# A third pair of blocks of K of u and v in seven products, the gating norm moved behind the scores, the spatial product behind half of the first gate

## The chip, the cores and the metric

The kernel runs on one core of one Trainium2 chip. The metric is the device time of one execution in microseconds (us). The kernel before took 512.1 us (median of 3 runs, 511.56 to 512.21). The engines are named as the profile names them: PE (TensorE: matmuls; PEld, its weight loads), DVE (VectorE), ACT (ScalarE), POOL (GpSimd) and SP (SyncE, which issues the DMAs).

## The reference

One residual block of a decoder on 256 tokens of width 1024, in f32: a SwiGLU FFN at half weight (hidden width 2816), a mixing layer, a second SwiGLU FFN at half weight, and a final RMS norm. The change lies in the mixing layer:

```python
n = rmsnorm(h, mix_norm)
z = n @ w_in                      # q, k, v (512 each), u and gv (512 each)
attn = moba_attention(q, k, v)    # 256 tokens, one block: causal softmax attention, 8 heads of 64
zg = gelu(z[..., 1536:])          # u, gv
gm = u * (W_s @ layernorm(gv) + b)   # per group of 64 channels, inside chunks of 128 tokens
gates = sigmoid(n @ w_gate + b_gate)
merged = gates[..., :D] * (attn @ w_branch_attn) + gates[..., D:] * (gm @ w_branch_gmlp)
h = h + merged @ w_out
```

In the kernel's units "u" is the first half of zg, "v" is the attention's v, and "gv" is the second half of zg, which gets the layer norm and the spatial product.

## The kernel before, in words

**Products.** Every weight matrix is read from HBM in f32 and split on the chip into a high part (a cast on ACT, L266) and a low part (a subtraction on DVE, L268). A product of a 128x128 block of activations with 512 columns of weights is then three matmuls into one PSUM bank (`mm3`, L261 to L263). Weights come in *units* of 1 MB, fetched by SP as two halves of 512 KB into 7 raw buffers (`fetch`, L186) and split into one of 5 split buffers (tag "w"). `split_to(n)` splits up to unit n and sets the fetches of the halves behind it going; `unit(i, ahead)` makes sure that the units up to i + ahead are split. The program's order in ACT, DVE, PE and SP is the order of the code in this part of the kernel (L758 on stands under `in_order()`, and PE's and SP's order is manual everywhere). So a split that is written earlier in the code stands earlier in DVE's queue.

**Seven products for eight.** For 2 blocks of K, 2 halves of the tokens and 2 halves of 512 columns, 8 products are needed. `seven` (L393) makes them from 7, in the manner of Strassen and Winograd: sums of quarters of the weights (`quarter_sums`, L200: four additions on DVE) and sums of blocks of the activations (`make_forms`, L411: four DVE operations, a cast on ACT, a low part on DVE). The weights of such a pair are two units: "single" (3 blocks of 512 columns) and "sums" (4 blocks), so 7 blocks are split from the 4 that are fetched. `chunk_pair` (L421) runs the pairs of a product, puts their results together (L437 to L441), and its `rest` multiplies the blocks of K that are left in the plain way (L443 to L453).

**The stretch around the change**, in PE's order: the first halves of K for q, k and gv (the second half of h is still on its way); their second halves; u and v together, of whose 8 blocks of K four are in two pairs (`PAIR_UV`) and four are plain, in units "u" and "v"; the scores of the attention; the spatial product (L925); then the eight units of the gate weights (four products g of two units each, `chunk(mg, ...)`). Beside it DVE and ACT split the units ahead, turn q and k by 32x32 transposes and a way through DRAM (L851 to L855, `from_way`), norm gv (`layer_norm`, L972, written ahead of u and v), add the masks (L876), and do the softmax (L879 to L907), whose probabilities go through DRAM as well (`to_keys`, `by_keys`). Later come the attention's product (`attend`, L960), the branch products with the gates (`merge`, L1077), whose results go through DRAM to the output projection (`down_features`, L1111).

**Queues.** While q and k are on their way, `hold[0] = 2 * mg` keeps SP from fetching gate weights; after the reads of the turned q and k it is lifted (L999), and the gate fetches stand behind those reads in SP's queue. A raw buffer comes free when the low part (or the last quarter sum) that reads it is done.

Of the kernel before, what the change touches and what calls it, by code (L numbers as in the profile page):

```python
# [18 lines left out]
P = 128  # L19
D = 1024  # L20
S = 256
# [25 lines left out]
WARM = 17  # L47
PAIR = {"f1": 6, "f2": 6}
PAIR_K = 3
PAIR_UV = 2  # L50


@with_exitstack
def block_kernel(ctx, tc, t, out):
# [84 lines left out]
    units.extend((name, i) for i in range(2) for name in ("q", "k", "gv"))  # L139
    muv = len(units)  # L140
    units.extend(("uvs", i, what) for i in range(PAIR_UV) for what in ("single", "sums"))
    units.extend([("u", 0), ("v", 0)])
    mg = add_units("gate", 8)
    mb = len(units)
    units.extend([("bg", 0), ("ba", 0), ("bg", 1), ("ba", 1)])
# [42 lines left out]
    def split_half(later=False):  # L188

        i, hf = divmod(done_to[0], 2)  # L190
        if hf == 0:
            unit_tile(i)
        fetch_to(done_to[0] + RAW)
        done_to[0] += 1
        if kind(i):
            return quarters(i, hf)
        w, sl = parts[i], half(i, hf)
        return split(w[:, sl, 0, :], w[:, sl, 1, :], raws.pop((i, hf)), later)

# [7 lines left out]
        nc.vector.tensor_add(second[:, 0], first[:, 0], d)  # L207
        nc.vector.tensor_add(second[:, 1], second[:, 0], c)

    def quarters(i, hf):  # L210

        w = parts[i]
        if kind(i) == "single":
            r = raws[i, hf].rearrange("p one (n c) -> p (one n) c", c=512)
            r, to = (r, w[:, 1:3]) if hf else (r[:, :1], w[:, :1])
        else:
            if hf == 0 and (i, 0) not in raws:
                quarter_sums(i)
            r, to = raws.pop((i, hf)), w[:, 2 * hf:2 * hf + 2]
        return split(to[:, :, 0, :], to[:, :, 1, :], r)  # L220

    def split_to(n):
        while done_to[0] < 2 * min(n, len(units)):
# [41 lines left out]
    def split(hi, lo, src, later=False):  # L265
        nc.scalar.copy(hi, src)  # L266
        def rest():
            nc.vector.tensor_sub(lo, src, hi.bitcast(F32))  # L268
        return rest if later else rest()
# [151 lines left out]
            between()  # L421
        low()

    def chunk_pair(name, at, nT, forms, ahead):


        acc, shared = {}, {}

        def tokens_of(k, j):
            return tuple(p[:, j * P:(j + 1) * P] for p in block_of(nT, k))  # L430

        for i in range(len(forms)):
            seven(name, at + 2 * i, i, tokens_of, acc, shared, forms[i], i == len(forms) - 1, ahead)
        p1, p5, p6, p7 = (shared[n,] for n in (1, 5, 6, 7))
        to = [sump.tile([P, NT, 512], F32, tag="sum", name=f"{name}{e}") for e in range(2)]
        (c00, c10), (c01, c11) = ([x[:, j] for j in range(NT)] for x in to)
        nc.scalar.copy(c00, p1)  # L437
        nc.vector.tensor_add(c01, p6, c00)
        nc.vector.tensor_add(c10, p7, c01)
        nc.vector.tensor_add(c11, p5, c10)  # L440
        nc.vector.tensor_add(c01, p5, c01)  # L441

        def rest(e, ahead=ahead):  # L443
            at_rest, near = at + 2 * len(forms), KB - 2 * len(forms)
            w = unit(at_rest + e * (near == 4), ahead)
            for k in range(near):
                for j in range(NT):
                    product(acc, name, (j, 512 * e), tokens_of(KB - near + k, j),
                            tuple(w[:, (2 * e + k) % 4 if near == 2 else k, two, :] for two in range(2)), k == near - 1)
            for j in range(NT):  # L450
                x = to[e][:, j]
                (nc.vector.tensor_sub if e else nc.vector.tensor_add)(x, acc[j, 512 * e], x)
            return [to[e][:, j] for j in range(NT)]  # L453
        return rest
# [303 lines left out]
    with in_order():  # L758
# [54 lines left out]
            if n == len(f1d) - 3:  # L813
                norm_parts(0)

        uv_forms = act.tile([P, 2, 4, 2, P], F32R, tag="nD", name="uvforms")
        uv_normed = sump.tile([P, 4, S // 32, 32], F32, tag="sum", name="uvnormed")
        hold[0] = 2 * mg
        psq = chunk(mq, nT2, "q", 0, [0], apart=3)
# [4 lines left out]
        psk = chunk(mk, nT2, "k", 0, [0], apart=3)  # L824
        for k in range(4):
            nc.scalar.activation(uv_normed[:, k], h_block(k), AF.Identity, scale=gain2[:, k:k + 1])
        for i in range(PAIR_UV):
            rest = split_half(True)
            make_forms(lambda j, k: uv_normed[:, 2 * i + k, 4 * j:4 * j + 4, :], uv_forms[:, i], f"uvform{i}", rest)
        norm_parts(1)  # L830
        psgv = chunk(mgv, nT2, "gv", 0, [0], apart=3)
        mixed = act.tile([P, 2 * FB, S], F32, tag="aT", name="mixed")
        mix_a, mix_b = mixed[:, :FB], mixed[:, FB:]
# [135 lines left out]
                                 start=False, stop=True)  # L969
            split(aoT[:, hp, 0, :], aoT[:, hp, 1, :], po[:, :S])  # L970

        def layer_norm(j):  # L972
            st = small.tile([P, 6], F32, tag="st", name=f"st{j}")
            nc.vector.bn_stats(st, gv[:, j, :])
            mvr = small.tile([P, 2], F32, tag="mvr", name=f"mvr{j}")
            nc.vector.bn_aggr(mvr, st)
            ve = small.tile([P, 1], F32, tag="ve", name=f"ve{j}")
            nc.vector.tensor_scalar(ve, mvr[:, 1:2], EPS, None, op0=ALU.add)
            r = small.tile([P, 1], F32, tag="lnr", name=f"lnr{j}")
            nc.gpsimd.tensor_tensor(r, ve, nhalf, op=ALU.pow)  # L980
            nc.vector.scalar_tensor_tensor(gv[:, j, :], gv[:, j, :], mvr[:, 0:1], lng, op0=ALU.subtract, op1=ALU.mult)
            nc.vector.scalar_tensor_tensor(gv[:, j, :], gv[:, j, :], r, lnb, op0=ALU.mult, op1=ALU.add)


        nc.sync.dma_start(lng, t["ln_g"].to_broadcast([P, GW]))
        nc.sync.dma_start(lnb, t["ln_b"].to_broadcast([P, GW]))
        chunk(mq, nT2, "q", 0, [1], psq, 3, DEEP)
        turn_qk(0, psq)
        chunk(mk, nT2, "k", 0, [1], psk, 3, DEEP)
# [1 line left out]
        quarter_sums(muv + 3)  # L991
        turn_qk(1, psk)
        nc.sync.dma_start(by_token(qk_way[1]), qk_turned[1])
        q_back = tmp.tile([P, S // 32, P], F32, tag="back", name="qback", bufs=1)
        from_way(q_back, qk_way[0])
        qk = act.tile([P, 2, 4 * S], F32, tag="nC", name="qk")
        kT = qk[:, 1].rearrange("p (q c) -> p q c", q=S // 32)
# [4 lines left out]
        for j in range(NT):  # L1002
            nc.scalar.activation(gv[:, j, :], psgv[j], AF.Gelu_apprx_tanh, scale=rs2[j])

        for j in range(NT):
            lows = [split_half(True) for _ in range(2)]
            layer_norm(j)
            for low in lows:
                low()
        qT = qk[:, 0].rearrange("p (k t) -> p k t", k=4)  # L1010
        nc.scalar.copy(qT.rearrange("p k (q c) -> p q k c", c=32), q_back.rearrange("p q (k c) -> p q k c", c=32))
        uv = chunk_pair("uv", muv, nT2, [uv_forms[:, i] for i in range(PAIR_UV)], DEEP)
        psu = uv(0)
        for j in range(NT):
            nc.scalar.activation(ut[:, j, :], psu[j], AF.Gelu_apprx_tanh, scale=rs2[j])
        psv = uv(1, ALONE)

        scores(0)
        scores(1)
        spatial()  # L1020
        psg = chunk(mg, nT2, "g", 0, [0])
        nc.sync.dma_start(gates[:, 0, :], t["b_gate"].to_broadcast([P, 2 * D]))

        sooner = act.tile([P, 2, 2, 512], F32, tag="nD", name="sooner")
# [172 lines left out]
def _packed(inputs):  # L1197
# [5 lines left out]
    def by_half(w):  # L1203
        return w.reshape(2, KB // 2, P, -1).transpose(0, 2, 1, 3)
# [30 lines left out]
    def paired(units, c):  # L1235
# [13 lines left out]
        "f1d": down1.reshape(FB, P, 2, 512)[REST].transpose(2, 0, 1, 3).reshape(PLAIN, 4, P, 512).transpose(0, 2, 1, 3),  # L1249
        "f2d": rows(a["ffn2_w_down"][0][hidden]),  # L1250
        "q": by_half(w_in[:, :AW][:, four]), "k": by_half(w_in[:, AW:2 * AW][:, four]),
        "v": by_half(w_in[:, 2 * AW:3 * AW])[1:],
        "u": by_half(w_in[:, 3 * AW:3 * AW + GW])[1:], "gv": by_half(w_in[:, 3 * AW + GW:]),
        "uvs": rows(np.concatenate([w_in[:, 3 * AW:3 * AW + GW], w_in[:, 2 * AW:3 * AW]], 1))[:PAIR_UV],
        "gate": chunks(a["w_gate"][0][order]),
        "ba": cols(a["w_branch_attn"][0], AW, 512), "bg": cols(a["w_branch_gmlp"][0][four], GW, 512),
# [26 lines left out]
```

## Time and profile before

| | |
|---|---|
| median of 3 runs | 512.1 us (511.56 to 512.21) |
| the profiled execution | 511.55 us, span of its instructions 509.8 us |
| PE busy | 502.2 us (99%), 2314 matmuls |
| DVE busy | 459.4 us (90%) |
| ACT busy | 313.1 us (61%) |
| POOL busy | 11.4 us (2%) |
| mean granted TensorE clock | 0.996 |
| HBM read | 113.26 MB, 248 GB/s over the span with the writes |

Times in the trace are us from the first instruction of the span. Busy PE is modelled: a matmul of 512 columns is shown with 389 ns and overlaps the next, so the distance between two starts is what one costs in a row. The stage table gives busy time of each engine between two times; what is missing to the stage's length is idle time.

### The profile page before, as it was taken

What the parts mean: (1) busy time and instruction counts of PE and PEld (TensorE: products, weight loads), DVE (VectorE), ACT (ScalarE), POOL (GpSimd) and SP (SyncE); (2) the same over time, 40 slices, a digit from 0 to 9 for tenths busy, and PEclk for the clock granted to TensorE, in tenths of its full rate; (3) what the DMA queues carried; (4) which work ended last, traced back from release to release, by engine and by line L of the source; (5) the groups of instructions that cost most, each with busy time, mean ns of one, the idle gap of its engine ahead of it and who ended that gap; (6) DMA issues with size and microseconds to landing.
All of it is one profiled execution on the core that took longest, in us unless ns stands there. A gap on an engine that the chain in (4) does not pass through costs nothing.

```text
span 509.8 us, 6828 instructions
## 1 busy us (share of the span) xinstructions
PE 502.2 (99%) x2314; PEld 416.9 (82%) x2314; DVE 459.4 (90%) x674; ACT 313.1 (61%) x452; POOL 11.4 (2%) x25
## 2 busy tenths in 40 slices
PE   8999999999999999999999999999999999999995
PEld 6888888888888888888888888888888888888884
DVE  6898999999997988999995657998989999999995
ACT  7985549646573775866984603767726656565533
POOL 0010000001000010000000000001000000000001
PEclk9999999999999999999999999999999999999998
DMA  8998587798865878497899655927799659998502
GB/s 316 375 328 343 140 294 236 279 307 279 242 208 204 256 309 299 139 358 244 291 284 315 225 164 172 314 97 265 256 278 302 214 150 273 351 333 242 184 1 82
DMA packets 63986, 126.82 MB, mean 249 GB/s; under 512 B 11728, under 2 KB 36816, under 8 KB 63824
## 3 DMA queue, kind: packets, MB, share of 16 engines
q1 hardware_dynamic: 63664, 126.08, 74.7%
q8 instruction: 18, 0.29, 0.2%
q10 hardware_dynamic: 288, 0.31, 0.2%
q14 instruction: 16, 0.13, 0.1%
HBM read 113.26 MB, written 13.11 MB: 248 GB/s over the span
## 4 chain that ended last, share of the span: by engine, by line
PE 97%; DMA 1%; DVE 0%; issue 0%; ACT 0%; POOLq 0%; DVEq 0%; POOL 0%; ACTq 0%
PE f L261 12%; PE f L262 12%; PE f L263 12%; PE accdown L263 4%; PE accdown L262 4%; PE accdown L261 4%; PE acch L262 4%; PE acch L261 4%; PE acch L263 4%; PE acc L235 3%; PE g L261 3%; PE g L262 3%; PE g L263 3%; PE acc L240 1%; PE accuv L262 1%; PE accuv L263 1%
## 5 line engine op out<-in xcount | busy, mean ns | idle before, releaser
L268 DVE TENSOR_TENSOR w<-raw,w 128x1024 fp32r<-128x1024 f32 (+1 forms) x176 | 198.2, 1162 | 10.1 <-ACT w L266 9.8
L266 ACT CAST w<-raw 128x1024 fp32r<-128x1024 f32 (+1 forms) x176 | 169.3, 1007 | 23.7 <-PE f L263 7.0
L263 PE MATMUL f<-w,n 128*128 128x512 f32 x272 | 105.8, 389 | 0.0
L261 PE MATMUL f<-w,n 128*128 128x512 f32 x272 | 105.8, 389 | 0.0
L262 PE MATMUL f<-w,n 128*128 128x512 f32 x272 | 105.8, 389 | 0.0
L263 PEld LDWEIGHTS f<-w,n 128*128 128x128 f32 x272 | 51.1, 188 | 10.6
L261 PEld LDWEIGHTS f<-w,n 128*128 128x128 f32 x272 | 51.0, 188 | 10.6
L262 PEld LDWEIGHTS f<-w,n 128*128 128x128 f32 x272 | 51.0, 188 | 10.6
L266 ACT CAST w<-sum 128x1024 fp32r<-128x1024 f32 x34 | 35.8, 1053 | 36.7 <-DVE sum L206 27.9
L268 DVE TENSOR_TENSOR w<-sum,w 128x1024 fp32r<-128x1024 f32 x34 | 40.9, 1215 | 0.5 <-ACT w L266 0.5
L261 PE MATMUL accdown<-w,f1h 128*128 128x512 f32 x68 | 26.5, 389 | 0.0
L262 PE MATMUL accdown<-w,f1h 128*128 128x512 f32 x68 | 26.5, 389 | 0.0
L263 PE MATMUL accdown<-w,f1h 128*128 128x512 f32 x68 | 26.5, 389 | 0.0
L261 PE MATMUL g<-w,n 128*128 128x512 f32 x64 | 25.0, 391 | 0.0
L263 PE MATMUL g<-w,n 128*128 128x512 f32 x64 | 24.9, 389 | 0.0
L262 PE MATMUL g<-w,n 128*128 128x512 f32 x64 | 24.9, 389 | 0.0
L261 PE MATMUL acch<-w,f2h 128*128 128x512 f32 x59 | 23.0, 389 | 0.0
L262 PE MATMUL acch<-w,f2h 128*128 128x512 f32 x59 | 23.0, 389 | 0.0
L263 PE MATMUL acch<-w,f2h 128*128 128x512 f32 x59 | 23.0, 389 | 0.0
L235 PE MATMUL acc<-mg,w 128*128 128x512 f32 x64 | 17.2, 393 | 0.0
L602 ACT ACTIVATE f2s<-f,rstd 128x256 f32<-128x256 f32 x18 | 8.2, 475 | 12.7 <-PE f L263 11.9
L266 ACT CAST mg<-mixed 128x256 fp32r<-128x256 f32 x8 | 2.8, 403 | 21.1 <-DMA mixed<-mway 21.1
(294 smaller groups left out, 933.2 us busy)
## 6 DMA issues: line engine op xcount, KB each, us to landing
raw<-in_f SPq DMA_DIRECT2D x72, 512.0 KB, 6.2
raw<-in_f2d SPq DMA_DIRECT2D x22, 512.0 KB, 7.1
raw<-in_gate SPq DMA_DIRECT2D x16, 512.0 KB, 6.3
raw<-in_f1s SPq DMA_DIRECT2D x14, 512.0 KB, 6.0
raw<-in_f1d SPq DMA_DIRECT2D x14, 512.0 KB, 5.2
raw<-in_out SPq DMA_DIRECT2D x8, 512.0 KB, 6.0
raw<-in_f2s SPq DMA_DIRECT2D x6, 512.0 KB, 6.0
f1way<-f1t SPq DMA_DIRECT2D x11, 256.0 KB, 6.6
```

Of the source, the lines that this page charges most:

```text
L235: nc.tensor.matmul(ps, st, both.rearrange("p two n -> p (two n)"), start=first, stop=last)
L240: nc.tensor.matmul(ps[:, n:], st, both[:, 0, :], start=False, stop=False)
L261: nc.tensor.matmul(ps, sh, mh, start=first, stop=False)
L262: nc.tensor.matmul(ps, sh, ml, start=False, stop=False)
L263: nc.tensor.matmul(ps, sl, mh, start=False, stop=last)
L266: nc.scalar.copy(hi, src)
L268: nc.vector.tensor_sub(lo, src, hi.bitcast(F32))
L602: nc.scalar.activation(sg, ps[j][:, :CH], AF.Silu, scale=rs[j])
```

## The change

Three of the four pairs of blocks of K of u and v are made with seven products (`PAIR_UV = 3`). The third pair's scaled input blocks ("uvlast") come from the second half of h, after `norm_parts(1)`; its forms ("uvforms2") are made after the first "single" unit is split, in a tile of tag "back"; q's return, which had that tag, goes to a part of the tile "mixed". The plain rest of u and v is one unit "uv" with two blocks for each, in place of two units. The third pair's units are split where the norm of gv stood; the norm itself now stands behind the scores, in an order in which both token halves take the same step one after the other. Within u and v only gate 0 is split ahead (`end=1` keeps the last pair and the rest from splitting further), where gates 0 to 2 were; gates 1 to 3 are split with the first half of gate product 0. The spatial product stands behind that half.

```diff
-PAIR_UV = 2
+PAIR_UV = 3
...
     units.extend(("uvs", i, what) for i in range(PAIR_UV) for what in ("single", "sums"))
-    units.extend([("u", 0), ("v", 0)])
+    units.append(("uv", 0))
...
-    def chunk_pair(name, at, nT, forms, ahead):
+    def chunk_pair(name, at, nT, forms, ahead, end=DEEP):
...
         for i in range(len(forms)):
-            seven(name, at + 2 * i, i, tokens_of, acc, shared, forms[i], i == len(forms) - 1, ahead)
+            seven(name, at + 2 * i, i, tokens_of, acc, shared, forms[i], i == len(forms) - 1,
+                  end if i == len(forms) - 1 else ahead)
...
-        for i in range(PAIR_UV):
+        for i in range(2):
             rest = split_half(True)
-            make_forms(lambda j, k: uv_normed[:, 2 * i + k, 4 * j:4 * j + 4, :], uv_forms[:, i], f"uvform{i}", rest)
+            make_forms(lambda j, k: uv_normed[:, 2 * i + k, 4 * j:4 * j + 4, :], uv_forms[i], f"uvform{i}", rest)
         norm_parts(1)
+        uv_last = sump.tile([P, 2, S // 32, 32], F32, tag="sum", name="uvlast")
+        for k in range(2):
+            nc.scalar.activation(uv_last[:, k], h_block(4 + k), AF.Identity, scale=gain2[:, 4 + k:5 + k])
...
-        def layer_norm(j):
+        def layer_norm_factors(j):
...
+            return mvr, r
+
+        def layer_norm(factors):
+            for j, (mvr, r) in enumerate(factors):
+                nc.vector.scalar_tensor_tensor(gv[:, j, :], gv[:, j, :], mvr[:, 0:1], lng, op0=ALU.subtract, op1=ALU.mult)
+            for j, (mvr, r) in enumerate(factors):
+                nc.vector.scalar_tensor_tensor(gv[:, j, :], gv[:, j, :], r, lnb, op0=ALU.mult, op1=ALU.add)
...
+        uv_forms.append(tmp.tile([P, 4, 2, P], F32R, tag="back", name="uvforms2", bufs=1))
+        split_to(muv + 1)
+        make_forms(lambda j, k: uv_last[:, k, 4 * j:4 * j + 4, :], uv_forms[2], "uvform2")
         chunk(mq, nT2, "q", 0, [1], psq, 3, DEEP)
...
-        q_back = tmp.tile([P, S // 32, P], F32, tag="back", name="qback", bufs=1)
+        q_back = mix_a[:, :4].rearrange("p a (q c) -> p (a q) c", c=P)
...
-        for j in range(NT):
-            lows = [split_half(True) for _ in range(2)]
-            layer_norm(j)
-            for low in lows:
-                low()
+        split_to(muv + 2 * PAIR_UV)
...
-        uv = chunk_pair("uv", muv, nT2, [uv_forms[:, i] for i in range(PAIR_UV)], DEEP)
-        psu = uv(0)
+        uv = chunk_pair("uv", muv, nT2, uv_forms, DEEP, 1)
+        psu = uv(0, 1)
...
-        psv = uv(1, ALONE)
+        psv = uv(1, 1)
 
         scores(0)
         scores(1)
+        layer_norm([layer_norm_factors(j) for j in range(NT)])
+        psg = chunk(mg, nT2, "g", 0, [0])
         spatial()
-        psg = chunk(mg, nT2, "g", 0, [0])
```

The packing of the inputs on the host changes with it (the array "uv" in place of "u" and "v").

## Rows read from the trace of the kernel before

**Rows 1.** The page's busy shares of the engines, and the list of waits of PE (who waited for whom: total us, times, longest).

```profile
PE 502.2 (99%) x2314; PEld 416.9 (82%) x2314; DVE 459.4 (90%) x674; ACT 313.1 (61%) x452; POOL 11.4 (2%) x25
...
PE warm L105 <- DVE zeros L102: 1.2, 1, 1.2
PE f L704 <- ACT n L680: 0.4, 1, 0.4
```

**Rows 2.** The stage table: stretch, its length, and for each engine busy us and instructions; then granted clock, share of the DMA engines and GB/s.

```profile
core 0: us, PE busy (x) PEld busy (x) DVE busy (x) ACT busy (x) POOL busy (x), PEclk, DMA share, GB/s
197.00:213.30 16.30, 16.30 (x73) 13.51 (x72) 15.82 (x21) 11.23 (x15) 0.00 (x0) 1.00 0.55 208
213.30:233.30 20.00, 20.00 (x90) 16.52 (x88) 18.85 (x25) 12.12 (x14) 1.96 (x2) 1.00 1.03 335
233.30:240.40 7.10, 7.10 (x60) 5.96 (x59) 7.10 (x13) 5.88 (x10) 0.00 (x0) 1.00 0.51 175
240.40:256.80 16.40, 16.40 (x74) 13.59 (x73) 15.90 (x27) 16.34 (x47) 0.00 (x0) 1.00 0.86 289
256.80:282.00 25.20, 25.20 (x114) 20.60 (x112) 17.86 (x18) 14.45 (x18) 0.00 (x0) 1.00 0.98 307
...
290.30:306.80 16.50, 16.50 (x86) 14.13 (x84) 10.85 (x15) 2.72 (x4) 0.00 (x0) 1.00 0.54 168
```

**Rows 3.** PE's work for u and v: of the groups by line, those of the first of the three matmuls (the other two lines have the same counts), and rows of PE's timeline (start us, us, instruction): two neighbours at the start of u and v, the scores and the spatial product.

```profile
L261 PE MATMUL accuv<-w,n 128*128 128x512 f32 x22 | 8.6, 389 | 0.0
L261 PE MATMUL accuv<-w,uvforms 128*128 128x512 f32 x8 | 3.1, 389 | 0.0
...
213.09 0.39 PE L261 MATMUL accuv<-w,n 128*128 128x512 f32 x1
213.32 0.39 PE L262 MATMUL accuv<-w,n 128*128 128x512 f32 x1
...
233.58 2.89 PE L869 MATMUL sc<-qk 64*128 64x128 f32 x32
236.40 2.05 PE L925 MATMUL mix<-mixed,wsT 128*128 128x128 f32 x16
```

**Rows 4.** DVE's timeline from the forms of the second pair to the softmax (start us, us, instruction and how many in a row, and idle time ahead with what ended it).

```profile
191.09 0.29 DVE L415 TENSOR_TENSOR uvform<-uvnormed 128x128 f32<-128x128 f32 x1
...
192.03 1.22 DVE L268 TENSOR_TENSOR w<-raw,w 128x1024 fp32r<-128x1024 f32 x1
...
199.30 0.69 DVE L205 TENSOR_TENSOR sum<-raw 128x512 f32<-128x512 f32 x1
...
201.83 2.43 DVE L268 TENSOR_TENSOR w<-sum,w 128x1024 fp32r<-128x1024 f32 x2
...
209.63 1.30 DVE L855 STREAM_TRANSPOSE mixed<-mixed 128x512 f32<-128x512 f32 x2
...
213.33 0.69 DVE L974 BATCH_NORM_STATS2 st<-mixed 128x6 f32<-128x512 f32 x1 [0.16 <-ACT mixed L1003]
...
215.52 0.75 DVE L982 SCALAR_TENSOR_TENSOR mixed<-mixed,lnr 128x512 f32<-128x512 f32 x1 [0.43 <-POOL lnr L980]
...
235.64 2.60 DVE L876 TENSOR_TENSOR mixed<-sc,mask 128x512 f32<-128x512 f32 x6
...
240.43 1.21 DVE L881 TENSOR_REDUCE mx<-mixed 128x8 f32<-128x1024 f32 x1
...
254.52 2.31 DVE L906 STREAM_TRANSPOSE turned<-mixed 128x2048 f32<-128x2048 f32 x1 [0.19 <-ACT mixed L897]
```

**Rows 5.** ACT's timeline: four scalings of the forms' input, the table load ahead of gelu, gelu, and the casts of the two halves of gate 0 with their waits for the fetch.

```profile
186.54 1.71 ACT L826 ACTIVATE uvnormed<-h,cols 128x256 f32<-128x256 f32 x4
...
210.82 1.28 ACT L1003 ACT_TABLE_LOAD   x1
212.61 1.37 ACT L1003 ACTIVATE mixed<-gv,rstd 128x512 f32<-128x512 f32 x2 [0.50 <-PE gv L263]
...
220.89 1.06 ACT L266 CAST w<-raw 128x1024 fp32r<-128x1024 f32 x1 [2.18 <-DMA raw<-in_gate]
222.55 1.05 ACT L266 CAST w<-raw 128x1024 fp32r<-128x1024 f32 x1 [0.61 <-DMA raw<-in_gate]
```

**Rows 6.** SP's timeline: the write of the turned k, the four reads of it, and the gate fetches behind them (start of the first, us to the end of the last).

```profile
210.96 0.38 SPq L993 DMA_DIRECT2D qkway<-mixed  x1
...
214.15 1.78 SPq L576 DMA_DIRECT2D qk<-qkway  x4
216.03 24.83 SPq L186 DMA_DIRECT2D raw<-in_gate  x15
```

**Rows 7.** Timelines of ACT, DVE and PE from the third gate's end to the output projection: the cast of the second half of the later branch weight, the addition of gate 3, the low parts of the attention output, the last transposes of the first merged half, the cast and the low part of what returns from DRAM, and the first matmuls of the output projection.

```profile
277.34 1.06 ACT L266 CAST w<-raw 128x1024 fp32r<-128x1024 f32 x1 [0.17 <-DMA raw<-in_bg]
...
282.06 1.54 DVE L943 SCALAR_TENSOR_TENSOR mixed<-g,rstd,mixed 128x512 f32<-128x512 f32 x2 [1.93 <-PE g L263]
284.55 1.42 DVE L268 TENSOR_TENSOR ao<-po,ao 128x256 fp32r<-128x256 f32 x4 [0.96 <-ACT ao L266]
...
297.42 0.71 DVE L1096 STREAM_TRANSPOSE mt<-mixed 128x512 f32<-128x512 f32 x1
...
305.41 0.71 ACT L266 CAST mg<-mixed 128x256 fp32r<-128x256 f32 x2 [12.88 <-DMA mixed<-mway]
...
305.85 0.76 DVE L268 TENSOR_TENSOR mg<-mixed,mg 128x256 fp32r<-128x256 f32 x2 [4.88 <-ACT mg L266]
...
306.80 0.63 PE L235 MATMUL acc<-mg,w 128*128 128x512 f32 x2
```

More of the change, by code (lines that the diff above doesn't have):

```diff
@@ L195, in split_half @@
         if kind(i):
-            return quarters(i, hf)
+            return quarters(i, hf, later)
         w, sl = parts[i], half(i, hf)
@@ L208, in quarter_sums, with quarters @@
         nc.vector.tensor_add(second[:, 1], second[:, 0], c)
-    def quarters(i, hf):
+    def quarters(i, hf, later=False):
         w = parts[i]
@@ L219, in quarters @@
             r, to = raws.pop((i, hf)), w[:, 2 * hf:2 * hf + 2]
-        return split(to[:, :, 0, :], to[:, :, 1, :], r)
+        return split(to[:, :, 0, :], to[:, :, 1, :], r, later)
     def split_to(n):
@@ L814, in block_kernel @@
                 norm_parts(0)
-        uv_forms = act.tile([P, 2, 4, 2, P], F32R, tag="nD", name="uvforms")
+        uv_two = act.tile([P, 2, 4, 2, P], F32R, tag="nD", name="uvforms")
+        uv_forms = [uv_two[:, 0], uv_two[:, 1]]
         uv_normed = sump.tile([P, 4, S // 32, 32], F32, tag="sum", name="uvnormed")
@@ L980, in layer_norm @@
             nc.gpsimd.tensor_tensor(r, ve, nhalf, op=ALU.pow)
-            nc.vector.scalar_tensor_tensor(gv[:, j, :], gv[:, j, :], mvr[:, 0:1], lng, op0=ALU.subtract, op1=ALU.mult)
-            nc.vector.scalar_tensor_tensor(gv[:, j, :], gv[:, j, :], r, lnb, op0=ALU.mult, op1=ALU.add)
+            return mvr, r
[4 more added lines that the diff above has]
+                nc.vector.scalar_tensor_tensor(gv[:, j, :], gv[:, j, :], r, lnb, op0=ALU.mult, op1=ALU.add)
         nc.sync.dma_start(lng, t["ln_g"].to_broadcast([P, GW]))
         nc.sync.dma_start(lnb, t["ln_b"].to_broadcast([P, GW]))
+        uv_forms.append(tmp.tile([P, 4, 2, P], F32R, tag="back", name="uvforms2", bufs=1))
+        split_to(muv + 1)
+        make_forms(lambda j, k: uv_last[:, k, 4 * j:4 * j + 4, :], uv_forms[2], "uvform2")
         chunk(mq, nT2, "q", 0, [1], psq, 3, DEEP)
@@ L1251, in _packed @@
         "q": by_half(w_in[:, :AW][:, four]), "k": by_half(w_in[:, AW:2 * AW][:, four]),
-        "v": by_half(w_in[:, 2 * AW:3 * AW])[1:],
-        "u": by_half(w_in[:, 3 * AW:3 * AW + GW])[1:], "gv": by_half(w_in[:, 3 * AW + GW:]),
+        "uv": np.concatenate([by_half(w)[1:, :, 2:] for w in (w_in[:, 3 * AW:3 * AW + GW], w_in[:, 2 * AW:3 * AW])], 2),
+        "gv": by_half(w_in[:, 3 * AW + GW:]),
         "uvs": rows(np.concatenate([w_in[:, 3 * AW:3 * AW + GW], w_in[:, 2 * AW:3 * AW]], 1))[:PAIR_UV],
```

## The prediction

> **What bounds the kernel now.** I read the page's busy shares first and then the list of what TensorE (PE) waits for [rows 1]. PE is busy 502.2 of 509.8 us and has only two waits, 1.2 and 0.4 us, both before the first product. From there it runs matmul behind matmul: PE sets the end, a matmul removed saves its spacing, and a wait that opens on PE is added in full. The spacing is the difference of two starts in the timeline: 213.32 - 213.09 = 0.227 us [rows 3].
>
> The stage table [rows 2] says how much cover the other engines have. The reader is to see VectorE (DVE): idle 0.5 us in 197.0 to 213.3, 1.15 in 213.3 to 233.3, 0 in 233.3 to 240.4, 0.5 in 240.4 to 256.8. So DVE hides behind PE with 2.1 us to spare in 60 us, because it works ahead. Only later is there room: 7.3 us in 256.8 to 282.0 and 5.65 in 290.3 to 306.8. The change adds DVE work at 197, where the room is missing.
>
> **Part 1, what is removed.** A pair of blocks of K of u and v was 8 products of 3 matmuls and becomes 7. The trace has 3 x (22 + 8) = 90 matmuls of 512 columns for u and v [rows 3], and 87 are left: 3 x 0.227 = **-0.68 us**. The bytes fetched stay the same (eight halves of 512 KB).
> By the Trainium skill, "TensorE: Matmul & The Clock Gate", section "Back-to-back issue gap", a stream of weight loads and matmuls settles at about 131 ns per 512 columns; the saving would be 0.39 us. The trace does not agree (227 ns), and the measured spacing decides.
>
> **Part 2, what is added on DVE**, at the spacings of the same operations [rows 4]: four form operations 0.94 (191.09 to 192.03) and their low part 0.65; four quarter sums 2.53 (199.30 to 201.83); low parts of seven blocks where four were, 3 x 0.57 = 1.7 (two of 128x1024 take 2.43 overlapped, so 1.14 to 1.2 each, half of that a block). Together **5.8 us**. ScalarE gets two scalings of 0.41 [rows 5], a cast of 0.6 and casts of three blocks; it has idle time there [rows 2], so its own work costs nothing, but its order makes DVE wait. The forms' new tile and the moved tile for q's return take space that is free by then, and nothing waits for it.
>
> **Part 3, DVE's new order, added up.**
> - Up to the transposes of k (209.63 before): the two scalings stand ahead of the first cast, +0.85; form +1.0; DVE waits 0.65 for the form's cast, which ScalarE can start only after the fourth form operation; low part 0.65. **+3.15**, so 212.8.
> - SyncE's queue hangs on these: the write of k (210.96) goes at 214.1, the reads of it (214.15 to 215.93) end at 219.2, and the raw fetches behind them start at 219.3 instead of 216.03 [rows 6]. First of them is now the second half of the shared u/v unit, which reaches its turn only here; gate 0 is behind it.
> - gelu's table load stood idle before (210.82, gelu at 212.61 [rows 5]). Now the casts of the sums end at 214.0, the table takes 1.3, gelu 1.35, and the third pair's first cast ends at 217.15. DVE, free at 216.4, waits 0.8 + 0.35; low parts 1.75, sums 2.53, low parts 2.3: 224.2. PE wants the pair's second unit at 213.09 + 51 x 0.227 = 224.65, and its first half is ready at 223.1. Covered.
> - The shared unit: DVE waits 0.8 (q's copy of 1.05 and one cast are ahead on ScalarE), 2.3 of low parts: 227.2. Its halves are wanted at 227.4 and 230.1 and are ready at 226.2 and 227.3: covered by 1.2 us.
> - Gate 0: before, its halves were there at 220.8 and 222.5, 4.8 and 6.5 us after the issue at 216.03 [rows 5, 6]. From 219.3, with one half of 1.3 us ahead, they land at 225.4 to 225.9 and 226.7 to 228.1; its low parts end at 229.5 to 230.4.
> - Four sums of the pairs 2.65, u 1.2, v 1.2, masks 2.5 (2.60 before): **237.1 to 238.0**. It was 238.2 before, but then gates 1 and 2 and the norm were done.
> - The norm of v, now here: 2 x 2.43 (213.33 to the end of the row at 215.52, less its wait of 0.43): **242.0 to 242.9**. The low parts of gates 1 to 3, 6 x 1.14: 248.8 to 249.7. Only then the first maximum of the softmax, 240.43 before: **8.4 to 9.3 us late**.
>
> **Part 4, what PE meets.** u and v end at 213.09 + 87 x 0.227 = 232.8; scores 2.9 (233.58 to 236.40, and the gap ahead): 235.7; half of gate 0, 24 x 0.227 = 5.44: 241.15. Moving the spatial product behind that half adds no matmul.
> - **Spatial product** waits for the norm, and all of PE's later work stands behind it: 0.9 to 1.8 us; taken 1.7 (before, gate 0's second half came 1.7 after its first, not 1.3).
> - **Gate 5**: the last transposes of the softmax (254.52 to 256.8) come at 263 to 263.8, the low parts behind them at 265.2 to 266.0, the first half ready at 267.3 at the late end; PE wants it at 241.15 + 1.7 + 2.0 + 96 x 0.227 = 266.6. Between 0 and 0.7, taken 0.6.
> - **Products of the attention branch**: the late transposes go out by DMA, and SyncE issues the gating product's way out, its return and the next branch weights behind them. All of these move by the same 8.4 to 9.3. The branch weight behind which gate 3's addition stands on DVE landed at 277.3 (start of its cast [rows 7]); now at 286. That addition (282.06, when it waited for PE) falls to 288.3, the split of the attention output (284.55) to 291, ready at 292.5. PE wants it at 290.3 - 0.7 + 2.3 = 291.9. Between 0 and 1.2, taken 0.7.
> - **Output projection**: here the kernel before has no slack at all. The last transpose of the first merged half ends at 298.13, goes by DRAM, is cast at 305.41, its low part ends at 306.6, and PE starts on it at 306.80 [rows 7]. Now DVE does the low parts of two units (4.6) and two gate products (1.35) between 292.5 and 298.4, then three operations of 2.1 in all, twice: 302.6 to 303. With the same 8.5 us by DRAM the low part ends at 311.1 to 311.8. PE would be there at 306.8 - 0.7 + 3.0 = 309.1. **2.0 to 2.7**, taken 2.5.
> The four waits are one backlog met four times: what an earlier one does not take, the last one does. Sum: 1.7 + 0.6 + 0.7 + 2.5 - 0.68 = **+4.8 us**. Bounds of this case: the last low part at 310.0 (part 3 at its short end, and 1 us less of waits) gives +3.2; at 313 (1 us more in the DMA queue) gives +6.2. Nothing after 306.8 gives it back, since PE has no wait there [rows 1].
> Against the profiled execution, 511.55 us (span 509.8 and 1.75 around it): 516.4. That execution lies at the low end of the runs (511.56 to 512.21, median 512.1), so the median should be 0.4 above: **516.8**, own range 515.2 to 518.4.
>
> **Rivals.**
> - *The change pays as it says: 511.4* (512.1 - 0.68). One place decides: the norm of v against the first half of gate 0. If DVE is done with the norm by 241.15, 1.7 us earlier than I have it, the spatial product doesn't wait, and the backlog behind it must then be under 4 us, which is what the later idle time of DVE takes up without the DRAM returns. For it: 5.44 us of matmuls are put there for 4.86 of norm. Against it: DVE starts the norm at 237 to 238 and not at 235.7, since the masks of the scores are ahead of it. Chance 0.12, of which 0.03 is faster by more than 0.2%.
> - *Only the early waits: 513.3.* The spatial product and gate 5 wait, 1.2 to 2.3 us in all, and the late chain catches up, as DVE's 7.3 us of idle time in 256.8 to 282.0 [rows 2] would allow if the returns by DRAM weren't in it: 512.1 - 0.68 + 1.2 to 2.3 is 512.6 to 513.7. Chance 0.19, of which 0.07 is within 0.2%.
> - *PE comes back slow: 518.5.* If a wait gets long and PE then runs some 3.4 us at half its rate, 7 or 8 matmuls are done there in place of 15: +1.7 us on the forecast. In the trace the granted clock is 1.00 in every stage [rows 2], but no stage has a wait to test it. My largest wait is 2.5. Chance 0.06.
> The last one goes with a rule of the Trainium skill, "TensorE: Matmul & The Clock Gate", section "Why this matters for your kernels": PE idle for more than about 3 us falls back to half clock. No row of the trace shows it.
>
> **How the numbers follow.** Forecast 0.63, rivals 0.12, 0.19 and 0.06. A difference of 0.2% (1.0 us) is about what a measurement here can tell from none. Slower by more: 0.63 + 0.12 + 0.06 = 0.81; within: 0.09 + 0.07 = 0.16; faster: 0.03. The range leaves out the first rival, the short end of the second and a tail at the top: 512.9 to 518.8.
>
> **What would show it.** Right: PE's list of waits gains an entry at the spatial product for the norm, 1 to 2 us near 241, and one at the first matmuls of the output projection for the merged half, 2 to 3 us; the first maximum at 249 to 250; the gate fetches from 219.3; 87 matmuls for u and v. Wrong: PE without a wait there, or the masks done on DVE before 236, which would mean that DVE's waits of part 3 are not there. A wait at the scores for a bank of u or v, or at the third pair, would mean that a cover I counted on fails, and the time is above the range.

## The result, and the profile after

The changed kernel takes **515.0 us** (median of 4 runs) where the kernel before, timed beside it, takes 511.9 us: ratio 1.0076, 95% interval 1.0062 to 1.009. (The ratio is one of means, and one of the four runs took 518.2 us; the medians alone give 1.0061.) It is slower by 3.1 us. The forecast was a price of 4.8 us and a time of 516.8; its range of 512.9 to 518.8 holds the result, which lies just below the 515.2 to 518.4 given to the main case alone.

| | before | after |
|---|---|---|
| profiled execution, its span | 511.55, 509.8 us | 514.78, 513.1 us |
| PE busy | 502.2 us, 2314 matmuls | 503.0 us, 2311 matmuls |
| DVE busy | 459.4 us | 465.2 us |
| ACT busy | 313.1 us | 315.3 us |

The list of PE's waits after (who waited for whom: total us, times, longest) answers to [rows 1]:

```profile
PE acc L235 <- DVE mg L268: 1.6, 1, 1.6
PE warm L105 <- DVE zeros L102: 1.2, 1, 1.2
PE g L262 <- DVE w L268: 0.7, 1, 0.7
PE mix L930 <- DVE mixed L992: 0.3, 1, 0.3
PE f L705 <- ACT n L681: 0.2, 1, 0.2
```

Three entries are new: the output projection (acc), a gate product (g) and the spatial product (mix), each a single wait for DVE. The list counts from the modelled end of the matmul ahead (0.39 us behind its start, where the next one starts after 0.227), which lies later than the moment at which PE could have gone on. The price of a wait is therefore read from starts, as the distance to the start before, less the usual spacing. PE's timeline after, at the three places (start us, us, instruction, idle time ahead and what ended it):

```profile
241.29 0.39 PE L263 MATMUL g<-w,n 128*128 128x512 f32 x1
241.97 0.79 PE L930 MATMUL mix<-mixed,wsT 128*128 128x128 f32 x5 [0.29 <-DVE mixed L992]
...
265.62 0.39 PE L261 MATMUL g<-w,n 128*128 128x512 f32 x1
266.76 0.50 PE L262 MATMUL g<-w,n 128*128 128x512 f32 x1 [0.75 <-DVE w L268]
...
307.80 0.28 PE L263 MATMUL pa<-w,ao 128*128 128x256 f32 x1
309.70 0.98 PE L235 MATMUL acc<-mg,w 128*128 128x512 f32 x3 [1.61 <-DVE mg L268]
```

Spatial product: 241.97 - 241.29 - 0.227 = 0.45. Gate unit 5: 266.76 - 265.62 - 0.227 = 0.91. Output projection: 309.70 - 307.80 - 0.12 (spacing of the 256-column matmuls) = 1.78. Together 3.1 us of waits, against 0.68 us saved. PE's last matmul ends 3.2 us later than before (507.02 for 503.80); what is left of that are small gaps, 0.3 of them in the output projection's stretch (22.68 us for 22.36 from its first matmul to the next product's), and a start on u and v that is 0.18 later.

DVE's timeline after answers to [rows 4]: the first of the third pair's forms, the last transposes of k, the masks, the norm (two statistics, two passes), the low parts of gates 1 to 3, the first maximum, the second turn of the softmax.

```profile
199.31 0.29 DVE L415 TENSOR_TENSOR uvform<-uvlast 128x128 f32<-128x128 f32 x1
...
211.96 1.30 DVE L860 STREAM_TRANSPOSE mixed<-mixed 128x512 f32<-128x512 f32 x2
...
234.33 2.83 DVE L881 TENSOR_TENSOR mixed<-sc,mask 128x512 f32<-128x512 f32 x6
237.08 0.68 DVE L979 BATCH_NORM_STATS2 st<-mixed 128x6 f32<-128x512 f32 x1
...
240.42 1.41 DVE L992 SCALAR_TENSOR_TENSOR mixed<-mixed,lnr 128x512 f32<-128x512 f32 x2
241.74 6.89 DVE L268 TENSOR_TENSOR w<-raw,w 128x1024 fp32r<-128x1024 f32 x6
248.56 1.21 DVE L886 TENSOR_REDUCE mx<-mixed 128x8 f32<-128x1024 f32 x1
...
263.29 2.31 DVE L911 STREAM_TRANSPOSE turned<-mixed 128x2048 f32<-128x2048 f32 x1 [0.66 <-ACT mixed L902]
```

The masks end at 237.16, 1.1 us sooner than before (235.64 + 2.60). But the norm (4.7 us) and the low parts of gates 1 and 2 (four of the six, 4.5 us), done by then before, now follow, and the maximum starts 8.1 us late (240.43 before). The second turn is late by 8.8.

How that reaches the output projection is read from SP's timeline after: the turned softmax goes to DRAM, its first read comes back, the turned gated product (done on DVE at 261.2) goes out behind it, then further reads, the return of the gated product, and only then the branch weights.

```profile
265.63 3.09 SPq L916 DMA_DIRECT2D on_way<-turned  x4
268.83 1.23 SPq L924 DMA_DIRECT2D mixed<-on_way  x1
270.10 1.59 SPq L1061 DMA_DIRECT2D gmway<-mixed  x2
272.34 0.85 SPq L924 DMA_DIRECT2D mixed<-on_way  x2
276.04 1.80 SPq L577 DMA_DIRECT2D gmback<-gmway  x4
277.88 0.93 SPq L186 DMA_DIRECT2D raw<-in_bg  x2
```

ACT after waits for these at 283.41 and 285.66, and DVE's addition of gate 3 stands behind both (timelines of ACT, then DVE, answering to [rows 7]):

```profile
283.41 1.05 ACT L266 CAST gm<-gmback 128x1024 fp32r<-128x1024 f32 x1 [3.14 <-DMA gmback<-gmway]
...
285.66 1.05 ACT L266 CAST w<-raw 128x1024 fp32r<-128x1024 f32 x1 [0.18 <-DMA raw<-in_bg]
```

```profile
284.49 1.23 DVE L268 TENSOR_TENSOR gm<-gmback,gm 128x1024 fp32r<-128x1024 f32 x1 [2.78 <-ACT gm L266]
285.63 2.35 DVE L268 TENSOR_TENSOR w<-raw,w 128x1024 fp32r<-128x1024 f32 x2
287.91 1.53 DVE L948 SCALAR_TENSOR_TENSOR mixed<-g,rstd,mixed 128x512 f32<-128x512 f32 x2
290.40 1.42 DVE L268 TENSOR_TENSOR ao<-po,ao 128x256 fp32r<-128x256 f32 x4 [0.96 <-ACT ao L266]
...
301.40 0.71 DVE L1106 STREAM_TRANSPOSE mt<-mixed 128x512 f32<-128x512 f32 x1
...
309.22 0.76 DVE L268 TENSOR_TENSOR mg<-mixed,mg 128x256 fp32r<-128x256 f32 x2 [4.26 <-ACT mg L266]
```

The lateness shrinks link by link: 8.3 us at the branch weight's cast (277.34 before), 5.85 at gate 3 and the attention output, 4.0 at the last transpose of the merged half, 3.4 at its low part, 2.9 at PE's first matmul of the output projection (306.80 before), of which the wait there is 1.78.

### The profile page after: what moved, and what is told of

Same layout as the page of the kernel before. It is cut to its first block, busy times and chain, and to the rows that moved or that the text cites. A ratio compares the mean times of both kernels' runs of the same rounds, so it can differ in the third digit from the quotient of the medians.

```text
span 513.1 us, 6839 instructions
## 1 busy us (share of the span) xinstructions
PE 503.0 (98%) x2311; PEld 416.5 (81%) x2311; DVE 465.2 (91%) x685; ACT 315.3 (61%) x457; POOL 10.9 (2%) x25
## 4 chain that ended last, share of the span: by engine, by line
PE 90%; ACT 3%; DMA 2%; DVE 2%; issue 1%; SPq 0%; POOLq 0%; DVEq 0%; POOL 0%; ACTq 0%
PE f L263 12%; PE f L261 12%; PE f L262 12%; PE accdown L263 4%; PE accdown L261 4%; PE accdown L262 4%; PE acch L262 3%; PE acch L261 3%; PE acch L263 3%; PE acc L235 3%; PE acc L240 1%; ACT mixed L891 1%; PE accf2p L262 1%; PE accuv L262 1%; PE accf1p L263 1%; PE accf1p L261 1%
## 5 line engine op out<-in xcount | busy, mean ns | idle before, releaser
L266 ACT CAST w<-sum 128x1024 fp32r<-128x1024 f32 x36 | 37.9, 1052 | 40.5 <-DVE sum L206 31.4
L268 DVE TENSOR_TENSOR w<-sum,w 128x1024 fp32r<-128x1024 f32 x36 | 43.4, 1216 | 0.5 <-ACT w L266 0.5
```

## The experiments

All are timed beside the kernel before (medians 511.7 to 511.9 us). Theory: the change puts 9.2 us of VectorE's work (the norm, the low parts of gates 1 and 2) behind the masks; from there one late chain runs through softmax, SP's queue and the merged half to the output projection. Rivals: the third pair's own work makes the lateness, and without it the order is free; each wait has a cause of its own; the row maxima's start decides.

**1. The order without the pair** (`two_pairs_new_order`). The kernel before with

```diff
-        for j in range(NT):
-            lows = [split_half(True) for _ in range(2)]
-            layer_norm(j)
...
+        split_to(muv + 2 * PAIR_UV)
-        uv = chunk_pair("uv", muv, nT2, [...], DEEP)
-        psu = uv(0)
+        uv = chunk_pair("uv", muv, nT2, [...], DEEP, 2)
+        psu = uv(0, 2)
-        psv = uv(1, ALONE)
+        psv = uv(1, 1)
-        spatial()
+        layer_norm([layer_norm_factors(j) for j in range(NT)])
         psg = chunk(mg, nT2, "g", 0, [0])
+        spatial()
```

> The order of the change without its third pair: the kernel before with two pairs, but the gating norm behind the scores, the spatial product behind half of the first gate, and only gate unit 0 split ahead of the scores. Theory 'third pair': VectorE only falls behind because the third pair brings it 6 to 7 us of added work before the scores; without that work it is ahead by then, so the scores' row maxima start at about 243 (240.4 before, 248.6 after the change) and the time is 511.5 to 512.5. Rival 'order': norm and gate splits behind the scores are late by themselves; the maxima start at 246 or later, PE waits again at the spatial product and at the output projection, and the time is 514 to 515.

Measured: 515.1 us, ratio 1.0061 (1.0046 to 1.0075). The rival "order" holds. DVE's timeline of this kernel, and behind it the two waits for DVE in its list of PE's waits:

```profile
218.62 4.63 DVE L268 TENSOR_TENSOR w<-raw,w 128x1024 fp32r<-128x1024 f32 x4 [5.89 <-ACT w L266]
...
233.87 1.37 DVE L453 TENSOR_TENSOR uv<-accuv,uv 128x512 f32<-128x512 f32 x2 [4.07 <-PE accuv L263]
235.64 2.89 DVE L877 TENSOR_TENSOR mixed<-sc,mask 128x512 f32<-128x512 f32 x6 [0.39 <-PE sc L870]
...
243.10 6.90 DVE L268 TENSOR_TENSOR w<-raw,w 128x1024 fp32r<-128x1024 f32 x6
249.91 1.22 DVE L882 TENSOR_REDUCE mx<-mixed 128x8 f32<-128x1024 f32 x1
```

```profile
PE acc L235 <- DVE mg L268: 0.9, 1, 0.9
PE mix L926 <- DVE mixed L988: 0.3, 1, 0.3
```

DVE now idles 10 us ahead of the masks. That helps nothing: the masks wait for PE's scores, and the norm and the splits stand behind the masks. The maxima start at 249.9 with two pairs, where three had 248.6. Most of what I had told as the third pair's price is the price of the order. Not quite all of it is shown to be: by starts the waits here are 0.45 us at the spatial product, 0.25 at gate unit 5 and 1.0 at the output projection, 1.7 in all where the change has 3.1. From the first product of u and v to the last of PE's this execution takes 293.30 us, that of the change 293.75, that of before 290.71. So the order alone makes 2.6 of the change's 3.0 us there, and the pair with the order gains nothing of its 0.68. The times of 515.1 and 515.0 us are too close to tell the two kernels apart.

**2. The pair without the order** (`three_pairs_old_order`). The change with norm, splits and spatial product back in their old places:

```diff
         split_to(muv + 2 * PAIR_UV)
+        layer_norm([layer_norm_factors(j) for j in range(NT)])
-        uv = chunk_pair("uv", muv, nT2, uv_forms, DEEP, 1)
-        psu = uv(0, 1)
+        uv = chunk_pair("uv", muv, nT2, uv_forms, DEEP)
+        psu = uv(0)
-        psv = uv(1, 1)
+        psv = uv(1, ALONE)
-        layer_norm([layer_norm_factors(j) for j in range(NT)])
-        psg = chunk(mg, nT2, "g", 0, [0])
         spatial()
+        psg = chunk(mg, nT2, "g", 0, [0])
```

> The third pair alone: norm ahead of the u and v products, spatial product directly behind the scores, gate units split ahead, as before. Theory 'third pair': VectorE has 4.8 us of norm and some 4.6 us of gate splits more to do before PE may go on behind the u and v sums, and PE waits there, early: 517 to 520. If the new order is what costs, this kernel is at 511 to 513 (8 matmuls of 128 x 512 by 0.227 us less, nothing added); if PE has slack enough ahead of the scores, it is no slower than the change, 514 to 515.

Measured: 520.9 us, ratio 1.0163 (1.0144 to 1.0182), the dearest of all and a little above the 517 to 520 expected. (The "8 matmuls" of the expectation should read 3.) PE's timeline shows the scores in three pieces. The second and the third wait for DVE, whose sums (L439) stand behind the norm and eight low parts:

```profile
235.67 0.48 PE L874 MATMUL sc<-qk 64*128 64x128 f32 x2 [0.42 <-DMA raw<-in_gate]
238.29 3.79 PE L874 MATMUL sc<-qk 64*128 64x128 f32 x22 [2.14 <-DVE uv L439]
243.21 1.73 PE L874 MATMUL sc<-qk 64*128 64x256 f32 x8 [1.13 <-DVE uv L453]
244.87 3.67 PE L930 MATMUL mix<-mixed,wsT 128*128 128x128 f32 x16
```

Beside the waits the 16 spatial products take 3.3 us (244.87 to 248.18) for 1.8 before; the last section comes back to that. So the pair in the old order costs 9 us and the order alone 3.2; both together cost 3.1. The order is the smaller price, paid so that the pair can come in.

**3. Two microseconds moved forward** (`factors_early`). The norm's statistics directly behind gelu:

```diff
+        factors = [layer_norm_factors(j) for j in range(NT)]
         split_to(muv + 2 * PAIR_UV)
...
-        layer_norm([layer_norm_factors(j) for j in range(NT)])
+        layer_norm(factors)
```

> The change, with the norm's statistics (VectorE 237.08 to 239.09, 2.0 us) put right behind the gelu of gv, where VectorE waits 0.74 us at 216.2, 0.67 at 224.0 and 0.62 at 226.9; only the passes over gv stay behind the scores. Theory 'VectorE is 8 us late and all waits come of it': everything from the norm on is up to 2.0 us earlier, the waits at the spatial product (0.6) and at gate unit 5 (0.9) go, the one at the output projection (1.8) falls by what the chain gains: 512.0 to 513.3. Rival 'transfers': the waits behind the scores are set by the fetch queue and not by VectorE; no more than the 0.6 of the spatial product goes: 514.2 to 515.

Measured: 513.0 us, ratio 1.0019 (1.0007 to 1.0032). 2.0 us forward, 2.0 us gained (1.9 from the first product of u and v to PE's last, 291.88 for 293.75). The waits at the spatial product and at gate unit 5 are gone from PE's list, that at the output projection is down to 0.9, with a small one behind it:

```profile
PE acc L235 <- DVE mg L268: 0.9, 1, 0.9
PE acc L235 <- DVE mixed L1105: 0.2, 1, 0.2
```

**4. SP's order alone** (`return_sooner`). No work less on any engine; the gated product goes out and comes back ahead of softmax's first reads:

```diff
         gate_in(0, psg)
+        for j in range(NT):
+            nc.sync.dma_start(by_token(gm_way)[:, j], gm_turned[j])
         turn(1)
         to_keys(1)
...
+        gm_back = tmp.tile(...)
+        from_way(gm_back, gm_way)
         by_keys(0)
-        (the write to gm_way; behind by_keys(1): gm_back and its read)
```

> The change, with the turned gated product written to DRAM ahead of the second stretch of softmax (it is done by 262, and is written at 270.1 because its issue stands behind the softmax's writes and first reads on SP), and read back ahead of those reads. Nothing is taken from any engine. Theory 'late chain through SP': the return lands near 275 to 277 in place of 283.3, ScalarE and VectorE no longer idle for it before gate unit 3, the attention output's low parts come before 288 in place of 290.4, the merged half is turned 2 us earlier or more and the wait of 1.8 at the output projection goes: 512.9 to 513.6. Rival 'VectorE alone': what is late at the output projection is late because VectorE has too much to do, not because of the order on SP: 514.6 to 515.2.

Measured: 513.6 us, ratio 1.0037 (1.0023 to 1.0052). SP's timeline, to be held against the one of after:

```profile
262.37 0.91 SPq L1053 DMA_DIRECT2D gmway<-mixed  x2
265.51 3.23 SPq L916 DMA_DIRECT2D on_way<-turned  x4
270.02 2.50 SPq L577 DMA_DIRECT2D gmback<-gmway  x4
272.62 2.74 SPq L924 DMA_DIRECT2D mixed<-on_way  x3
275.40 0.91 SPq L186 DMA_DIRECT2D raw<-in_bg  x2
```

DVE turns the softmax no sooner (263.17), yet the return's issue is 6.0 us sooner, gate 3's addition 1.9 (286.00), and no wait at the output projection is left in PE's list. So the last wait comes by way of SP's queue, and not from DVE having too much to do there. Where the lateness starts is another matter: it is DVE's late softmax that stands ahead in that queue, and experiment 3 shortens the same wait from that end.

**5. Both mends** (`factors_and_return`: the diffs of 3 and 4).

> Both earlier edits of the change together: the norm's statistics behind the gelu of gv, and the gated product's return ahead of softmax's first reads. Alone they gave 513.0 and 513.6 where the change has 515.0. Theory 'one late chain, two links': the first edit takes the waits at the spatial product (0.6) and gate unit 5 (0.9), the second the one at the output projection (1.8, of which the first left 0.9); with both, none is left ahead of the output projection, and what the third pair saves (3 products of 0.227 us, 0.7) remains less some 0.3 in the output projection's own stretch: 511.3 to 511.9. Rival 'the same wait counted twice': what the two edits gain is the same time, and the pair stands at 512.8 to 513.2.

Measured: 511.3 us, ratio 0.9991 (0.9983 to 1.0). Its list of PE's waits holds the start-up entry alone:

```profile
PE warm L105 <- DVE zeros L102: 1.2, 1, 1.2
```

From the first product of u and v to the last of PE's it takes 290.05 us (213.44 to 503.49) where before took 290.71: 0.66 us less, about the 0.68 of three matmuls.

**6. Once more, beside a twin with two pairs** (`factors_and_return_again`, `two_pairs_factors_and_return`: the kernel of experiment 1 with the same two diffs).

> The three pairs with both mends once more, beside its two-pair twin on the same chip: 511.1 to 511.5, with a ratio to the kernel before of 0.998 to 1.000. If the first measurement was chance: 511.7 or more.

> The kernel before with two pairs, in the change's order with both mends (statistics early, return ahead of softmax's first reads). Theory 'order and pair are separate': the order's own price of 3.2 us (two pairs in the new order, unmended) goes with the mends, and nothing is gained over the kernel before: 511.6 to 512.2; the three pairs in the same order stand 0.3 to 0.8 below it (3 products of 0.227 us). Rival 'the order gains by itself': 511.3 or less, level with the three pairs, so that the pair is worth nothing.

Measured: three pairs 511.7 us, ratio 0.9998 (0.999 to 1.0007); two pairs 512.2 us, ratio 1.0009 (0.9998 to 1.0019). The gain of experiment 5 over the kernel before did not come back: 511.7 lies above the 511.1 to 511.5 expected, at the value that stood for chance. The mends take the order's price away without the pair too. The three pairs stand 0.5 us below the two, but the intervals overlap. In PE's starts the pair's gain is seen: from the first product of u and v to PE's last it takes 290.05 us with three pairs, in this execution as in that of experiment 5, and 290.83 with two. It is too small for the clock time to prove, since in the profiled executions (that of experiment 2 aside) u and v themselves begin anywhere from 213.1 to 214.0 us. Against the kernel before, the best version is level or at most 0.2% ahead (the lowest bound of its two intervals is 0.9983).

**7. The maxima sooner** (`softmax_sooner`, `softmax_and_factors`, `maxima_first`). The first splits gate unit 1 alone ahead of the maxima, units 2 to 4 behind them, and moves the second turn ahead of the second gated product and the first gate's addition to the end; the second is that with the diff of 3; the third has only the first move:

```diff
-        psg = chunk(mg, nT2, "g", 0, [0])
+        psg = chunk(mg, nT2, "g", 0, [0], ahead=1)
...
-        lows = [split_half(True) for _ in range(2)]
+        two, three = [[split_half(True) for _ in range(2)] for _ in range(2)]
         sums = [exponents(j) for j in range(NT)]
+        (low parts of two)
         gated(0)
+        (low parts of three)
+        lows = [split_half(True) for _ in range(2)]
```

> The change with the same instructions on VectorE, but gate unit 1 alone split ahead of the scores' maxima; gate units 2, 3 and 4 are split where VectorE would wait for the exponents, the second stretch of softmax is turned ahead of the second gated product, and the first gate is added last. Theory 'late chain': the row maxima start 4.5 us sooner (244 in place of 248.6), the turned softmax 3 us or more sooner, the gated product's return and the fetches behind it on SP as much; the wait at the output projection goes, the one at gate unit 5 shrinks, the spatial product's 0.6 stays: 512.3 to 513.5. Rival 'sum of work': VectorE has the same work up to the attention output and is busy almost without a gap, so the order within it changes nothing: 514.6 to 515.3.

> The order of the kernel softmax_sooner together with the norm's statistics ahead of the pairs' splits. Theory 'late chain': with the statistics early the spatial product's wait goes too, and no wait over 0.3 us is left between the scores and the output projection: 511.3 to 512.0. Rival 'sum of work': no better than the statistics alone, 513.0.

> The change with one move: the row maxima of the scores ahead of the splits of gate units 2 and 3, which VectorE then does while ScalarE takes the exponents; all else as in the change (softmax_sooner moved three more things and made ScalarE wait for the first gate's sums). The maxima start near 244 in place of 248.6, but the same instructions stand ahead of the second softmax turn. Theory 'sum of work': VectorE has no idle time to give up there but the 0.7 us ahead of that turn, so the turn moves by 0.7 at most (262.6 to 263.3) and the time is 514.3 to 515.1. Rival 'late maxima': what counts is when the maxima start; the turn comes at 260 or sooner and the time is 512 to 513.5.

Measured: 515.7 us (ratio 1.0076, 1.0061 to 1.009), 513.1 us (1.0032, 1.0017 to 1.0046), 514.3 us (1.0061, 1.0042 to 1.0079). The first two missed: with the first gate's addition last, ACT's sigmoids waited for it and the casts of gate unit 5 behind them came too late for PE. ACT's timeline of `softmax_sooner`:

```profile
263.88 0.63 ACT L955 ACTIVATE mixed<-mixed 128x512 f32<-128x512 f32 x1 [4.90 <-DVE mixed L948]
...
266.42 3.88 ACT L266 CAST w<-raw 128x1024 fp32r<-128x1024 f32 x4
```

They tell nothing clean about the maxima. `maxima_first` does. DVE's timeline of it:

```profile
243.83 1.21 DVE L886 TENSOR_REDUCE mx<-mixed 128x8 f32<-128x1024 f32 x1
...
262.50 2.31 DVE L911 STREAM_TRANSPOSE turned<-mixed 128x2048 f32<-128x2048 f32 x1 [0.22 <-ACT mixed L902]
```

The maxima start 4.7 us sooner, the second turn 0.8, and the time falls by 0.7, which is within the intervals of the two kernels (1.0042 to 1.0079 and 1.0062 to 1.009) but far from the 1.5 to 3 us that the rival asked for. PE's list has lost the entry at gate unit 5 and still has 1.8 at the output projection. What counts is the sum of DVE's work ahead of the turn, as DVE is busy almost without a gap up to it.

**8. The spatial product undone** (`spatial_first`). In the change,

```diff
+        spatial()
         psg = chunk(mg, nT2, "g", 0, [0])
-        spatial()
```

> The change with one part undone: the spatial product directly behind the scores again, the norm still behind them. PE then has no product to do while VectorE norms gv: it waits from 235.9 to about 241.4, some 5.4 us, in one piece. Theory 'late chain': VectorE's work is not delayed by that, so PE's later waits (0.9 at gate unit 5, 1.8 at the output projection) are swallowed by the early one, and the time is 515.0 + 5.4 - 0.6 - 2.7 = 517.1, between 516.5 and 517.7. Rival 'waits add': each wait has its own cause and stays, 519.5 to 520. Rival 'PE comes back slow': after 5 us without work the products run at half their rate for some time (0.454 us for one in place of 0.227); for 3 us of that the time rises by another 1.5, and the first g products stand at over 0.4 us spacing.

Measured: 519.2 us, ratio 1.0146 (1.0133 to 1.016), 2 us above what the theory gave. PE's list has one wait there, 5.9 us, and none later, so the later ones were swallowed; "waits add" fails, though its number is close. The rival "PE comes back slow" has the missing part, though not in the g products, as it said: these come at 0.23 us again, and the slow ones are the spatial products. It is in PE's timeline and in the stage table (columns as in [rows 2]):

```profile
242.26 3.69 PE L930 MATMUL mix<-mixed,wsT 128*128 128x128 f32 x16 [5.91 <-DVE mixed L992]
245.70 0.48 PE L261 MATMUL g<-w,n 128*128 128x512 f32 x1
```

```profile
236.00:242.00 6.00, 0.36 (x4) 0.00 (x0) 5.76 (x14) 5.78 (x9) 1.52 (x2) 0.74 0.01 3
242.00:246.00 4.00, 3.74 (x17) 3.72 (x18) 4.00 (x5) 1.65 (x2) 0.00 (x0) 0.53 0.34 109
```

The 16 spatial products take 3.44 us (242.26 to 245.70) in place of 1.8, at a granted clock of 0.53 (1.00 from 246 to 250). Sum: 515.0 - 3.1 (the three waits) + 6.1 (the wait by starts) + 1.6 = 519.6, near the 519.2 measured. Moving the spatial product behind half of the first gate is what keeps PE from that; it is worth 4 us in this order.

## Why the prediction was right, and where not

- **Sign and mechanism: right.** PE sets the end, of 90 matmuls for u and v 87 are left (19.81 us from their first start to the scores, 213.27 to 233.08; 20.49 before), and waits open behind the scores that cost more than the three matmuls save.
- **Whose price it is: wrong.** Part 2 and the end of the first part put the lateness down to DVE work added where the room is missing. Experiment 1 has none of that work, and its softmax is as late. The order alone does it (9.2 us of work put behind masks that wait for PE); the pair's 5.8 us are for the most part hidden in what the order sets free. Part 3 holds the right cause in its own sum, as it lets the masks end no later than before and then counts 4.9 us of norm and 6.8 of low parts behind them, but it does not say that the order would be late without the pair.
- **Up to the transposes of k: +2.3 instead of +3.15.** The 0.85 for the two scalings failed: in this execution the last part of h was on the chip 0.8 us sooner, and they were done before the first cast was due. That is luck of the execution and no fault found in the sum: in `factors_and_return` they began 0.4 later, and the first cast was late by as much (197.02 for 196.58). The raw fetches began at 218.4 for 219.3. Hence 211.96 and not 212.8 for the transposes, and the steps behind it came out at their short ends or up to 0.2 below: gate 0's low parts ended at 229.4 (229.5 to 230.4), the masks at 237.2 (237.1 to 238.0), the norm at 241.8 (242.0 to 242.9), the maximum started at 248.6 (248.8 to 249.7).
- **Spatial product: mis-sized**, 0.45 for 1.7, and below the short end of 0.9 too. I took the long end for a term that is a difference of two times: the norm was done at 241.83 (242.9 at the long end), and PE was there at 241.52 and not at 241.15.
- **Gate 5: 0.9 for 0.6**, a little over its bound of 0.7, since PE came there at 265.85 and not at 266.6.
- **Products of the attention branch: 0 for 0.7.** The chain was as told (low parts at 290.40 for 291), and PE came when they were there.
- **Output projection: mis-sized**, 1.8 for 2.5, as the difference of two larger misses. The last transposes ended at 302.1 for 302.6 to 303, and the way by DRAM to the end of the low part took 7.9 us (302.1 to 310.0) for 8.5, so the low part ended 1.1 to 1.8 sooner than I had it; and PE, after shorter waits, was there at 307.9 for 309.1.
- **Sum of waits 3.1 for 5.5.** "One backlog met four times" holds in kind: experiment 8 shows an early wait swallowing the later ones. By that rule the sum hangs on the last low part alone, and this ended at 310.0, for which the prediction's own bounds give +3.2. What was too long is the late chain up to that point; the four single sizes follow from it and were taken near their long ends.
- **Rivals.** "Pays as it says" asked for a norm done by 241.15; it was done at 241.83, and experiment 3, where it is done at 240.2, loses that wait. "Only the early waits" failed: the biggest wait is the late one, by the returns through DRAM, as argued there (experiment 4). "PE comes back slow" did not happen in the change, where no wait is over 1.8 us and the granted clock stays at 1.00; it did in experiments 2 and 8.

Open: the pair's own gain in clock time (0.5 us measured, with overlapping intervals), and what sets the length of wait after which PE comes back slow.

## What to carry to other kernels

Work that is moved behind a step that waits for the bounding engine is late by its own length, however idle its engine is before that step; ask what the moved work stands behind, and not only whether its engine has time. When lateness shows far from its origin, follow it through the queue that issues the transfers: here a product was ready 9 us before its issue, and moving the issue forward gained 1.4 us (515.0 to 513.6) with no less work on any engine. And move a wait early only while PE has something else to do: one long wait can cost its length and a slow start behind it.

## What the runs showed of the hardware

- **Half rate after a long wait.** In experiment 8 the granted clock was 0.50 from 239.0 on, 2.8 us into a stretch of 6.1 us without a product, and still from 245.0 to 245.5; the spatial products came every 0.215 us, for 3.4 us, and not every 0.11. After the waits of 0.9 and 1.8 us in the change the next products came at the usual spacing, at a clock of 1.00. The Trainium skill, "TensorE: Matmul & The Clock Gate", section "Why this matters for your kernels", says to leave no gap of more than about 3 us between bursts; 1.8 and 6.1 us agree with it.
- **Several short waits can do the same.** In experiment 2 the granted clock fell twice. Behind waits of 0.4 and 2.1 us, with two small products between them, it was 0.50 from 239 to 241. From 242 to 245 it was 1.00 again, with a wait of 1.1 us in that stretch, and from 246 to 248 it was 0.50 once more, under the spatial products. So the length of one wait does not decide alone, as 1.8 us in the change did no harm; what does is not shown here.
- **The input's arrival wanders.** In four executions with the same code up to there ACT began the two scalings for the third pair at 194.42 (`softmax_sooner`), 194.73 (`factors_early`), 195.78 (after) and 196.22 (`factors_and_return`), as the last part of h came by DRAM. Sums of 0.4 to 0.9 us over steps that hang on such a transfer are within what one execution does by itself.
